# All gathered expert rows of the first tile and of the samples are traced ahead of the gates

## The chip, the core and the metric
The kernel runs on one core of one Trainium2 chip. The metric is device time of one execution in microseconds (us), of which the span, from the first to the last instruction in the trace, is nearly all. VectorE (DVE in the rows), ScalarE (ACT), TensorE (PE), GpSimd (POOL) and the sync engine (SP) each work through their own instructions in a fixed order and wait on semaphores for each other and for DMAs.

## What is computed
One layer of a decoder trunk, for a prompt of 512 tokens (four tiles of 128) and for 32 sample tokens: a projection, two groups of mixing heads, an output projection, and then an expert layer that gives every token 128 of 16384 experts. This last part is where the change lies:

```
def block(hb):
    q = (hb @ w_query).reshape(PEER_BLOCK, PEER_HEADS, 2, D_HALF)
    s = einsum('thcd,cnd->thcn', q, sub_keys)
    s1, i1 = top_k(s[:, :, 0], 16);  s2, i2 = top_k(s[:, :, 1], 16)
    ...                                   # the 16 best sums of s1 and s2: idx (128 per token), gate
    pre = einsum('td,tkd->tk', hb, eu[idx])
    act = gelu(pre) * gate
    return einsum('tk,tkd->td', act, ev[idx])
```

`eu` and `ev` have 16384 rows of 1024 floats each. A final norm gives `y_prompt` and `y_sample`.

## The kernel before
The four prompt tiles are numbered 0 to 3. Tiles 0 and 3 and the 32 samples compute the expert layer **by gathered rows**; tiles 1 and 2 compute it densely, against all 16384 experts.

Gathered rows (`experts`, called by `tile_experts` for a tile and `sample_experts` for the samples): for each k, GpSimd issues an indirect DMA that brings 128 rows of 1024 floats (one expert row to each partition, 512 KB) into one of six `gat` buffers, and VectorE uses it. A row of `eu` is multiplied with the token's vector and summed up (a **dot**: in the trace CUSTOM_DVE_ANT_0, and a short read of the sum into `pre`). After all dots ScalarE computes Gelu over `pre`, and then a row of `ev` is scaled by `act` and added to a running sum `x` (an **add**: SCALAR_TENSOR_TENSOR x<-gat,act,x). A tile has 128 dots and 128 adds. The samples are laid out as 4 groups of 32 tokens on the 128 partitions, so they have 32 dots and 32 adds, and at the end four additions of 32x1024, a norm and an output DMA. In the code `experts` is a generator: each `yield` is one row, and the list `side` holds the generators that are still to run. `beside(n)` adds n to what is due and takes that many steps of `side`.

Dense tiles (1 and 2): first **the gates**. `gates` is called once for each of the two tiles. For 16 groups of 8 tokens VectorE writes one-hot tables `uH` and `uL`, ScalarE scales columns of them into `vH` (line 1441), TensorE multiplies them (line 1444) into a 128x128 matrix of gates for each token, and ScalarE copies that out (lines 1533 and 1543 to 1545). Beside the gates runs `late()`, one step at a time: the output projection and the queries of tile 3 (TensorE, lines 1574 and 1596). Then **the blocks**: 128 of them, each with 128 experts. Each block takes 8 transposes of the `eu` block, 24 matmuls with the tokens, Gelu, the product with the gates, and 24 matmuls with the `ev` block into `acc`; VectorE makes the low halves `uL` and `aL` and the gate products, ScalarE the high halves, GpSimd the low half `vL` (line 1498). Beside the first blocks runs `late_heads()`: the top-16 searches for tile 3, on VectorE. When half of its heads are done it appends tile 3's gathered rows to `side`.

Ahead of the gates the samples' own expert search (`sample_heads`) and the search of tile 2 (`rest(2, dsel[1])`) run on VectorE and GpSimd (top-16 instructions, and products `ce` on GpSimd, line 1053), together with the attention of tile 3 (`attend(3)`).

Where a gathered row is traced is set by three numbers. `AHEAD = 280` steps are traced ahead of the gates: 257 are tile 0 (256 rows and its finish) and 23 belong to the samples. `RATE_G = 0.8` steps are traced after each of the 32 gate groups, 25.6 in all, and what is left goes to the blocks at `RATE_H = 1.6` and `RATE_D = 2.4` a block. The framework's scheduler then fixes the order on every engine; `tc.issue_after(marks[...])` only says that a row may not stand ahead of a given VectorE instruction. VectorE calls go through a recording wrapper, so nearly all of them show its line, 127.

Of the kernel before, what the change touches and what calls it, by code (L numbers as in the profile page):

```python
# [32 lines left out]
LAG = 2  # L33
WST = 3
UV = 5
AHEAD = 280
RATE_G = 0.8
RATE_D = 2.4
RATE_H = 1.6
LATE = 2  # L40
# [69 lines left out]
def bc(ap, shape):  # L110
    return ap.to_broadcast(shape)
# [3 lines left out]
def hymba_step(ctx, tc, x_prompt, x_sample, cache_k, cache_v, state_wkv, state_shift, meta, norm1_g, w_in, mu, w0,  # L115
# [4 lines left out]
    marks = []  # L120
# [124 lines left out]
    side, due = [], [0.0]  # L245

    def beside(n):

        due[0] += n
        while side and due[0] >= 1.0:  # L250
            due[0] -= 1.0
            if next(side[0], None) is None:
                side.pop(0)
        due[0] = min(due[0], 1.0)
# [949 lines left out]
    with ExitStack() as px:  # L1204
# [43 lines left out]
        def put(src, dst):  # L1248

            A.copy(dst[0], src)  # L1250
            V.tensor_tensor(dst[1], src, dst[0].bitcast(F32), OP.subtract)
# [171 lines left out]
    def gates(its, sel, ps, put):  # L1423


        i1T, i2T, gaT = sel
        its, iot = its
        ib = dt_("aH", 2, [128, 2, 128], BF16)
        for c, x in enumerate((i1T, i2T)):
            A.copy(ib[:, c], x)  # L1430
        for n, t8 in enumerate(range(0, 128, 8)):
            ob = dt_("uL", 2, [128, 128, GA], BF16)
            o0, o1 = dt_("uH", 2, [128, 8, 128]), dt_("vH", 2, [128, 8, 128])
            V.tensor_tensor(o0.rearrange("p t j -> p j t"), its, bc(ib[:, 0, t8:t8 + 8].unsqueeze(1), [128, 128, 8]), OP.is_equal)
            V.tensor_tensor(ob, its[:, :, 0:GA], bc(ib[:, 1, t8:t8 + GA].unsqueeze(1), [128, 128, GA]), OP.is_equal)
            for q0 in (0, 4):
                p = ps()
                for q in range(q0, q0 + 4):
                    t = slice(t8 + q, t8 + q + 1)
                    if q < GA:  # L1440
                        A.mul(o1[:, q, :], ob[:, :, q], gaT[:, t])
                    else:
                        V.tensor_scalar(o1[:, q, :], iot, i2T[:, t], gaT[:, t], OP.is_equal, OP.mult)
                    T.matmul(p[:, 128 * (q - q0):128 * (q - q0) + 128], o0[:, q, :], o1[:, q, :], start=True, stop=True)  # L1444
                put(t8 + q0, p)
            if n % LATE:
                next(more, None)
            with tc.issue_after(marks[-1]):
                beside(RATE_G)


    ND = 256
# [3 lines left out]
    def dt_(tag, bufs, shape, dt=F32):  # L1456
        return _t(dn, tag, bufs, shape, dt)
# [158 lines left out]
            yield True  # L1616
        coming[0] = False

    for n in range(AHEAD):
        with tc.issue_after(marks[gather_mark[0]]):  # L1620
            beside(1)
    more = late()
    its = one_hot_table()
    sels = [sel_transposed(0, dps, dt_("selT", 1, [128, 3, 128])), sel_transposed(1, dps, dt_("lsc", 1, [128, 3, 128]))]
    gates(its, sels[0], dps, stage)
    gates(its, sels[1], dps, keep)
    for _ in more:
        pass
# [71 lines left out]
```

## Time and profile before

| what | value |
|---|---|
| median of 3 runs | 2180.15 us (2161.02 to 2190.67) |
| the profiled execution, its own time | 2171.7 us |
| its span | 2169.9 us |
| TensorE busy | 1816.4 us (84%) |
| VectorE busy | 1639.2 us (76%) |
| GpSimd busy | 1271.9 us (59%) |
| ScalarE busy | 862.6 us (40%) |
[...]

All positions are microseconds from the start of the span. The stretches that matter here: the search of tile 2 and the attention of tile 3 up to about 1115, the gates from 1115 to 1248, the blocks from 1248 to about 2129, and the last adds of tile 3 up to the end.

### The profile page before, as it was taken

What the parts mean: (1) busy time and instruction counts of PE and PEld (TensorE: products, weight loads), DVE (VectorE), ACT (ScalarE), POOL (GpSimd) and SP (SyncE); (2) the same over time, 40 slices, a digit from 0 to 9 for tenths busy, and PEclk for the clock granted to TensorE, in tenths of its full rate; (3) what the DMA queues carried; (4) which work ended last, traced back from release to release, by engine and by line L of the source; (5) the groups of instructions that cost most, each with busy time, mean ns of one, the idle gap of its engine ahead of it and who ended that gap; (6) DMA issues with size and microseconds to landing.
All of it is one profiled execution on the core that took longest, in us unless ns stands there. A gap on an engine that the chain in (4) does not pass through costs nothing.

```text
span 2169.9 us, 37101 instructions
## 1 busy us (share of the span) xinstructions
PE 1816.4 (84%) x13915; PEld 1693.1 (78%) x13915; DVE 1639.2 (76%) x3285; ACT 862.6 (40%) x1975; POOL 1271.9 (59%) x951
## 2 busy tenths in 40 slices
PE   5999984585685868898567998999999999999992
PEld 5888973373574757798457988899999999999992
DVE  5643426679878988678989999867676767899988
ACT  6553421221132322433258943444444444444442
POOL 0110103678777677533824365768776777888885
PEclk9999986555675768799769999999999999999996
DMA  7532373487779789966859985789999998999987
GB/s 222 164 107 81 106 199 108 156 304 237 262 247 308 242 282 323 299 222 206 271 182 330 341 287 191 287 297 392 336 336 336 330 338 330 326 322 328 328 312 261
DMA packets 311306, 571.60 MB, mean 263 GB/s; under 512 B 32916, under 2 KB 194694, under 8 KB 310983
## 3 DMA queue, kind: packets, MB, share of 16 engines
q0 software_dynamic: 84048, 305.70, 39.6%
q1 hardware_dynamic: 227078, 263.53, 37.5%
q8 instruction: 110, 1.80, 0.3%
q14 instruction: 70, 0.57, 0.1%
HBM read 544.12 MB, written 25.65 MB: 263 GB/s over the span
## 4 chain that ended last, share of the span: by engine, by line
PE 56%; DVE 17%; issue 9%; DMA 8%; POOL 7%; ACT 3%; SPq 0%; POOLq 0%; DVEq 0%; ACTq 0%
PE acc L1523 5%; PE acc L1524 5%; PE acc L1522 5%; PE w L1508 5%; PE w L1505 5%; PE w L1506 5%; PE w L1491 4%; POOL gat L1075 4%; PE pD L220 3%; DVE x L127 3%; PE pD L966 2%; DVE gat L127 2%; DMA wst<-in_w_query_dram 2%; PE ps L220 2%; PE w L1444 2%
## 5 line engine op out<-in xcount | busy, mean ns | idle before, releaser
L127 DVE SCALAR_TENSOR_TENSOR x<-gat,act,x 128x1024 f32<-128x1024 f32 x287 | 440.5, 1535 | 12.5 <-DMA gat<-in_expert_v_dram,ei 9.4
L1075 POOL DMA_INDIRECT gat<-in_expert_u_dram,ei x256 | 337.0, 1316 | 132.2 <-DVE pre L127 45.8
L1075 POOL DMA_INDIRECT gat<-in_expert_v_dram,ei x256 | 317.7, 1241 | 122.6 <-issue 35.4
L1498 POOL TENSOR_TENSOR vL<-uv,vH 128x1024 fp32r<-128x1024 f32 x128 | 335.2, 2619 | 84.0 <-ACT vH L1497 82.7
L1522 PE MATMUL acc<-aH,vH 128*128 128x256 f32 x1024 | 292.2, 294 | 6.2 <-ACT aH L1514 6.2
L1523 PE MATMUL acc<-aL,vH 128*128 128x256 f32 x1024 | 289.5, 285 | 7.0 <-DVE aL L127 6.8
L1524 PE MATMUL acc<-aH,vL 128*128 128x256 f32 x1024 | 288.6, 284 | 0.0
L1505 PE MATMUL w<-dhH,uH 128*128 128x256 f32 x1024 | 251.6, 283 | 2.7 <-DVE uL L127 1.5
L1506 PE MATMUL w<-dhL,uH 128*128 128x256 f32 x1024 | 251.3, 283 | 0.0
L127 DVE CUSTOM_DVE_ANT_0 gat<-gat,h 128x1024 f32<-128x1024 f32 x160 | 202.7, 1279 | 44.7 <-DMA gat<-in_expert_u_dram,ei 41.7
L1523 PEld LDWEIGHTS acc<-aL,vH 128*128 128x128 f32 x1024 | 197.2, 193 | 8.9 <-DVE aL L127 8.8
L1505 PEld LDWEIGHTS w<-dhH,uH 128*128 128x128 f32 x1024 | 196.7, 192 | 3.1 <-DVE uL L127 1.7
L1522 PEld LDWEIGHTS acc<-aH,vH 128*128 128x128 f32 x1024 | 192.7, 192 | 7.1 <-ACT aH L1514 7.1
L1524 PEld LDWEIGHTS acc<-aH,vL 128*128 128x128 f32 x1024 | 197.1, 192 | 0.0
L1506 PEld LDWEIGHTS w<-dhL,uH 128*128 128x128 f32 x1024 | 196.7, 192 | 0.0
L1497 ACT CAST vH<-uv 128x1024 fp32r<-128x1024 f32 x128 | 134.9, 1054 | 148.9 <-issue 111.3
L127 DVE TENSOR_TENSOR uL<-w,uH 128x512 fp32r<-128x512 f32 x256 | 166.7, 682 | 10.1 <-ACT uH L1493 10.1
L127 DVE TENSOR_TENSOR w<-w,gl 128x128 f32<-128x128 f32 x128 | 50.3, 393 | 148.6 <-ACT w L1509 148.6
L127 DVE CUSTOM_DVE_ANT_0 gat<-gat,lx 128x1024 f32<-128x1024 f32 x128 | 158.1, 1268 | 0.0
L1508 PE MATMUL w<-dhH,uL 128*128 128x256 f32 x1024 | 148.1, 286 | 4.7 <-DVE uL L127 4.3
L1493 ACT CAST uH<-w 128x512 fp32r<-128x512 f32 x256 | 138.0, 593 | 8.0
L1508 PEld LDWEIGHTS w<-dhH,uL 128*128 128x128 f32 x1024 | 133.0, 192 | 7.6 <-DVE uL L127 6.9
(568 smaller groups left out, 4046.5 us busy)
## 6 DMA issues: line engine op xcount, KB each, us to landing
uv<-in_expert_u_dram SPq DMA_DIRECT2D x128, 512.0 KB, 4.5
uv<-in_expert_v_dram SPq DMA_DIRECT2D x128, 512.0 KB, 6.0
wst<-in_w_query_dram SPq DMA_DIRECT2D x48, 512.0 KB, 6.6
wst<-in_w_out_dram SPq DMA_DIRECT2D x24, 512.0 KB
wst<-in_w_in_dram SPq DMA_DIRECT2D x20, 512.0 KB, 4.4
h2T<-in_w_in_dram SPq DMA_DIRECT2D x20, 512.0 KB, 4.2
gscr<-uv SPq DMA_DIRECT2D x10, 1024.0 KB, 5.9
uv<-in_w_query_dram SPq DMA_DIRECT2D x8, 1024.0 KB, 12.2
```

The lines of the kernel that those rows point to most:

```text
L127: r = getattr(nc.vector, name)(*args, **kw)
L220: T.matmul(p[:, 0:n], w[:, k, :], x, start=(k == 0 and x is H and w is wH), stop=(k == 7 and w is wL))
L1075: G.indirect_dma_start(out=r, out_offset=None, in_=w[0], in_offset=bass.IndirectOffsetOnAxis(ap=ei[:, k:k + 1], axis=0))
L1493: A.copy(uH[:, ks, :], p)
L1497: A.copy(vH, vn)
L1498: G.tensor_tensor(vL, vn, vH.bitcast(F32), OP.subtract)
L1505: T.matmul(pre, uH[:, k, :], hH[:, k, :], start=(k == 0), stop=False)
L1506: T.matmul(pre, uH[:, k, :], hL[:, k, :], start=False, stop=False)
L1508: T.matmul(pre, uL[:, k, :], hH[:, k, :], start=False, stop=(k == 7))
L1522: T.matmul(o, vH[:, ds_], aH, start=(j == 0 and d % 2 == 0), stop=False, skip_group_check=True)
L1523: T.matmul(o, vH[:, ds_], aL, start=False, stop=False, skip_group_check=True)
L1524: T.matmul(o, vL[:, ds_], aH, start=False, stop=(j == 127), skip_group_check=True)
```

## The change
The constant `AHEAD` becomes "until nothing is left": all 257 steps of tile 0 and all 65 of the samples are traced before the first gate. After the gate groups no row is traced any more. The blocks' rates stay; since `side` is empty when they begin, they trace no row until `late_heads` appends tile 3.

```diff
-AHEAD = 280
-RATE_G = 0.8
 RATE_D = 2.4
 RATE_H = 1.6
...
             if n % LATE:
                 next(more, None)
-            with tc.issue_after(marks[-1]):
-                beside(RATE_G)
...
-    for n in range(AHEAD):
+    while side:
         with tc.issue_after(marks[gather_mark[0]]):
             beside(1)
     more = late()
```

Lines move up by two, and by four further down (a VectorE row shows L125 where it showed L127). On VectorE the two programs have the same order up to the 1326th row, which the trace has at about 1064 us. On TensorE the order is the same up to the blocks.

**First place, VectorE ahead of the gates.** Before, in the search of tile 2 (`sco`, `vals`, `cand` are its tiles) and the softmax of tile 3 (`sD`), no gathered row stands:

```order
L127 MATCH_REPLACE sco_1436_6944<-vals_7008,sco_1436_6944 128x128 x4
L127 TENSOR_TENSOR sD_7799<-sD_7799,sD_7804 128x4
L127 MATCH_REPLACE sco_1456_7044<-vals_7105,sco_1456_7044 128x128 x4
L127 MAX vals_7008<-sco_1436_6944 128x8 x4
L127 RECIPROCAL sD_7808<-sD_7799 128x4
L127 MAX vals_7105<-sco_1456_7044 128x8 x4
L127 MAX_INDEX idxu_7005<-vals_7008,sco_1436_6944 128x8 x4
```

Now a dot of the samples (the two ISA rows are the dot and the reading of its sum) stands between each two of these on VectorE:

```order
L125 MATCH_REPLACE sco_1436_6944<-vals_7008,sco_1436_6944 128x128 x4
L125 ISA gat_8780,pre_8703<-gat_8780,h_1918_8698 128x1024
L125 ISA pre_8703 128x1
L125 MATCH_REPLACE sco_1456_7044<-vals_7105,sco_1456_7044 128x128 x4
L125 ISA gat_8783,pre_8703<-gat_8783,h_1918_8698 128x1024
L125 ISA pre_8703 128x1
L125 TENSOR_TENSOR sD_7804<-sD_7797,snk 128x4
L125 ISA gat_8786,pre_8703<-gat_8786,h_1918_8698 128x1024
L125 ISA pre_8703 128x1
L125 MAX vals_7008<-sco_1436_6944 128x8 x4
```

Eleven dots, the product of `act`, the first scaling and 20 adds have moved into this stretch, all ahead of the first gate instruction.

**Second place, VectorE at the first gates.** Before, the last search rows (`ce`, `dsel`) are followed by the low halves of tiles 1 and 2 (`dhL`) and then by the one-hot tables:

```order
L127 TENSOR_TENSOR ce_7171<-iota_87,hl_7152 128x512
L127 TENSOR_REDUCE dsel_17_112<-ce_7171 128x32
L127 TENSOR_TENSOR dhL<-w_7873,dhH 128x4x128
L127 TENSOR_TENSOR dhL<-w_7880,dhH 128x4x128
L127 TENSOR_TENSOR dhL<-w_7889,dhH 128x4x128
L127 TENSOR_TENSOR dhL<-w_7896,dhH 128x4x128
L127 TENSOR_SCALAR vH_8792<-aL_8771,selT_8775 128x128 x2
L127 TENSOR_TENSOR uH_8791<-vL_8773,aH_8787 128x128x8
```

Now, on VectorE at the same place, adds of the samples stand between them, and some are left behind the first gate instruction:

```order
L125 TENSOR_TENSOR dhL<-w_7873,dhH 128x4x128
L125 SCALAR_TENSOR_TENSOR x_1953_8803<-gat_8859,act_8800,x_1953_8803 128x1024
L125 TENSOR_TENSOR dhL<-w_7880,dhH 128x4x128
L125 SCALAR_TENSOR_TENSOR x_1953_8803<-gat_8862,act_8800,x_1953_8803 128x1024
L125 TENSOR_TENSOR dhL<-w_7889,dhH 128x4x128
L125 TENSOR_TENSOR dhL<-w_7896,dhH 128x4x128
L125 TENSOR_SCALAR vH_8950<-aL_8929,selT_8933 128x128
L125 SCALAR_TENSOR_TENSOR x_1953_8803<-gat_8865,act_8800,x_1953_8803 128x1024
L125 TENSOR_SCALAR vH_8950<-aL_8929,selT_8933 128x128
L125 TENSOR_TENSOR uH_8949<-vL_8931,aH_8945 128x128x8
```

Eleven adds, the samples' four closing additions and their norm still stand among the groups of the first dense tile; where before 11 dots, the first scaling and 13 adds stood among both tiles' groups, none stands now among those of the second tile.

**Third place, VectorE in the first blocks.** Before, adds of the samples stand between the low halves and gate products of the blocks:

```order
L127 TENSOR_TENSOR uL_10185<-w_10186,uH_10184 128x512
L127 TENSOR_TENSOR uL_10185<-w_10193,uH_10184 128x512
L127 SCALAR_TENSOR_TENSOR x_2051_9243<-gat_10004,act_9240,x_2051_9243 128x1024
L127 TENSOR_TENSOR aL_10178<-w_10149,aH_10177 128x256
L127 SCALAR_TENSOR_TENSOR x_2051_9243<-gat_10066,act_9240,x_2051_9243 128x1024
L127 TENSOR_TENSOR w_10250<-w_10250,gl_10115 128x128
L127 TENSOR_TENSOR w_10250<-w_10250,gA_7907 128x128
```

Now VectorE has there only the blocks' own rows and the search of tile 3 (`lvals`, `lsc`, `lidx`):

```order
L125 TENSOR_TENSOR w_10228<-w_10228,gl_10194 128x128
L125 TENSOR_TENSOR w_10228<-w_10228,gA_7907 128x128
L125 TENSOR_TENSOR uL_10264<-w_10265,uH_10263 128x512
L125 TENSOR_TENSOR uL_10264<-w_10272,uH_10263 128x512
L125 TENSOR_TENSOR aL_10257<-w_10228,aH_10256 128x256
L125 MAX lvals_10666<-lsc_10664 128x8 x4
L125 MAX_INDEX lidx_10309<-lvals_10666,lsc_10664 128x8 x4
```

Eighteen adds and the samples' finish have left the blocks. GpSimd's and SP's queues move with them: the 64 gathers of the samples now all stand ahead of the first `vL` on GpSimd, and the output DMA of the samples stands on SP between the sixth and the seventh write of gates to `gscr`, where it stood among the blocks' loads. From about the 17th block on the rows of tile 3 stand at the same blocks as before.

## Rows read from the trace of the kernel before

**Rows 1.** Span and mean granted TensorE clock of the core.

```profile
core 0: 2169.9 us, clock 0.866
```

**Rows 2.** Busy time by stretch: PE, PEld, DVE, ACT, POOL, then PEclk, DMA share, GB/s.

```profile
670.00:960.00 290.00, 239.61 (x1433) 202.37 (x1433) 239.80 (x383) 91.37 (x229) 186.53 (x166) 0.74 0.86 284
...
1064.20:1115.10 50.90, 24.64 (x126) 19.87 (x124) 44.58 (x155) 12.23 (x32) 25.85 (x26) 0.60 0.62 193
...
1112.00:1180.00 68.00, 49.27 (x317) 45.37 (x318) 61.36 (x97) 56.75 (x141) 22.11 (x12) 0.86 0.83 277
1180.00:1248.00 68.00, 67.46 (x571) 65.02 (x570) 62.65 (x80) 64.46 (x231) 26.70 (x14) 1.00 0.95 327
1248.00:1400.00 152.00, 134.77 (x1065) 129.85 (x1064) 144.96 (x369) 64.93 (x123) 95.92 (x76) 0.97 0.71 249
1400.00:2100.00 700.00, 699.56 (x5904) 698.46 (x5903) 542.80 (x868) 295.35 (x530) 543.46 (x324) 1.00 0.91 333
```

**Rows 3.** What VectorE waited for from 1018 to 1112: us, times, longest.

```profile
DVE dsel L127 <- POOL ce L1053: 5.6, 4, 1.7
DVE gat L127 <- DMA gat<-in_expert_u_dram,eis: 2.7, 2, 2.2
```

**Rows 4.** Adds of tile 0, 670 to 960: busy us, mean ns, idle before.

```profile
L127 DVE SCALAR_TENSOR_TENSOR x<-gat,act,x 128x1024 f32<-128x1024 f32 x127 | 170.5, 1342 | 8.3 <-DMA gat<-in_expert_v_dram,ei 7.4
```

**Rows 5.** Dots of the samples from 1018 to 1112, grouped as above.

```profile
L127 DVE CUSTOM_DVE_ANT_0 gat<-gat,h 128x1024 f32<-128x1024 f32 x21 | 31.7, 1515 | 2.7 <-DMA gat<-in_expert_u_dram,eis 2.7
...
L127 DVE DVE_READ_ACCUMULATOR2_ANT pre<- 128x1 f32 x21 | 1.6, 78 | 0.0
```

**Rows 6.** Rows of the samples among the gates, 1112 to 1248.

```profile
L127 DVE SCALAR_TENSOR_TENSOR x<-gat,act,x 128x1024 f32<-128x1024 f32 x13 | 16.7, 1281 | 0.0
L127 DVE CUSTOM_DVE_ANT_0 gat<-gat,h 128x1024 f32<-128x1024 f32 x11 | 13.3, 1214 | 0.0
...
L127 DVE TENSOR_SCALAR x<-gat,act 128x1024 f32<-128x1024 f32 x1 | 0.7, 749 | 0.0
```

**Rows 7.** Rows of the samples among the blocks, 1248 to 1400.

```profile
L127 DVE SCALAR_TENSOR_TENSOR x<-gat,act,x 128x1024 f32<-128x1024 f32 x18 | 35.3, 1964 | 0.0
...
L127 DVE TENSOR_TENSOR h<-h,gat 32x1024 f32<-32x1024 f32 x3 | 4.8, 1584 | 0.4 <-DMA gat<-x 0.4
...
L127 DVE SCALAR_TENSOR_TENSOR gat<-h,sF,gat 32x1024 f32<-32x1024 f32 x1 | 1.3, 1262 | 0.0
```

**Rows 8.** GpSimd's low halves from 1248 to 1400.

```profile
L1498 POOL TENSOR_TENSOR vL<-uv,vH 128x1024 fp32r<-128x1024 f32 x19 | 46.8, 2464 | 18.2 <-ACT vH L1497 18.1
```

**Rows 9.** Gathers of the samples, 1018 to 1115: ns min/median/max, first and last start.

```profile
L1075 POOL DMA_INDIRECT gat<-in_expert_u_dram,eis x27: 934/981/2004, 1021.2 to 1087.1; - x27
...
DMA to landing us min/median/max: 4.3/5.6/9.5
```

**Rows 10.** What VectorE waited for from 1112 to 1180.

```profile
DVE uL L127 <- ACT vH L1441: 2.9, 2, 1.6
DVE act L127 <- ACT act L1089: 2.2, 1, 2.2
```

**Rows 11.** The chain that ended last, later gates: start us, us, what.

```profile
1207.80 1.79 PE w L1444 x16
1209.59 1.56 PE w L1596 x14
...
1211.37 2.15 PE w L1596 x18
```

**Rows 12.** Matmuls with the low half, 8 a block, 1264 to 1399.4.

```profile
L1508 PE MATMUL w<-dhH,uL x138: 274/283/388, 1264.6 to 1399.4; 128*128 128x256 f32 x138
```

**Rows 13.** The chain that ended last, two blocks behind 1399.

```profile
1399.44 0.96 PE w L1508 x8
...
1406.06 0.96 PE w L1508 x8
```

**Rows 14.** DMA issues of the page: count, KB each, us to landing.

```profile
uv<-in_w_query_dram SPq DMA_DIRECT2D x8, 1024.0 KB, 12.2
```

## The prediction
> **What bounds the kernel now.** I read the busy times by stretch first and asked of each stretch which engine is full. Between 1064 and 1115, the search of tile 2 ahead of the gates, VectorE is busy for 44.58 of 50.9 us and TensorE for half of it [rows 2]: VectorE sets the pace, and its few waits are for GpSimd's products and for gathered data, 5.6 and 2.7 us in the 94 us from 1018 [rows 3]. The first half of the gates (1112 to 1180) is mixed: VectorE 61.36, ScalarE 56.75, TensorE 49.27 of 68 us. The second half (1180 to 1248) is full on TensorE, 67.46 of 68 us at the whole granted clock, 1.00 [rows 2]; there the chain that ended last runs from matmul to matmul, gates (line 1444) and late queries (line 1596) by turns [rows 11]. In the first blocks (1248 to 1400) VectorE is full again, 144.96 of 152 us, and from 1400 to 2100 TensorE is, 699.56 of 700 us, with VectorE at 78% [rows 2]. So a gathered row costs time ahead of the gates, in the gates' first half at most partly, in their second half nothing, and in the first blocks time again.
>
> How much the first blocks lose can be counted. Two full blocks are 6.62 us apart [rows 13]. From 1264.6 to 1399.4 there are 138 of the matmuls that come eight to a block, 17 block distances and the start of one more [rows 12]. At full pace they would take 17 x 6.62 = 112.5 us; they took 134.8. **22.3 us** is what the blocks can give back at most.
>
> **The change part by part.** Up to the 1326th VectorE instruction nothing moves, so the first 1064 us stay.
>
> *Ahead of the gates.* Eleven dots come in at 1.515 + 0.078 us [rows 5], 17.5 us; the first scaling at 0.75 us [rows 6]; 20 adds, taken at the 1.342 us that tile 0's adds had beside similar work [rows 4], 26.8 us; the small product of `act`, some 0.2. Together 45.3 us on the engine that sets the pace here, where before the gathers of these rows waited. What can cover them is the 6.3 us that VectorE idles in this stretch [rows 2]: the adds now stand between a product and its sum, where the wait for GpSimd is. If all of it is filled, the stretch grows by 39 us; if VectorE is kept as busy as now (87.6%), by 45.3/0.876 = 52 us; if only as busy as from 670 to 960, where adds stood beside other work (239.8 of 290 us, 82.7%), the 89.9 us of both take 108.7, 58 us more. I take 93%, because the rows fill waits but bring waits for their data: 89.9/0.93 = 96.7, **+46 us**. Data should nearly keep up. 27 gathers were issued here before, the first at 1021 and each landing some 5.6 us later [rows 9]; some 31 more of 0.52 MB make 16 MB, and the stretch moved 193 GB/s at a DMA share of 0.62 [rows 2]. At 284 GB/s, as from 670 to 960, 10 + 16 MB take 92 us, just the stretch's new length. GpSimd's in-order queue must pass the gathers before the products `ce` behind them, and each gather waits until one of six buffers is free.
>
> *The gates.* Eleven dots (11 x 1.29 = 14.2 us), the scaling (0.75) and 13 adds (16.7) leave [rows 6]. Eleven adds (14.1), four additions and the norm's last product (4 x 1.5 + 1.3 = 7.3, at their prices in the blocks [rows 7]) come into the first half. In the first half that is +7 us of VectorE work, less the 2.2 us in which VectorE waited for the samples' Gelu and the 2.9 us for ScalarE's columns [rows 10], which other rows then fill. The second half loses adds on an engine that was not the bound. I take **0**, with +6 if the first half waits for VectorE alone, and -11 if it falls to ScalarE's 56.75 us. On SP the samples' output DMA waits for the end of that norm, and behind it wait a load of query weights and two writes of gates. The load takes 12.2 us [rows 14]; the scheduler has it beside the norm of tile 3, whose matmuls need the weights later, so it is at nothing here, 5 us if the norm comes late.
>
> *The blocks.* Eighteen adds leave at 1.964 us, 35.3 us, and the finish with 4.8 + 1.2 + 1.3 us [rows 7]: VectorE falls from 145 to 102 us over about 20 blocks, which need 132 us of TensorE. On average that is the 78% at which TensorE ran full later. It isn't spread evenly: tile 3's search remains, and it stands in the first 17 blocks. So not all of 22.3 us comes back; I take **-17 us**, between -10 and -22.
>
> That an add costs 1.96 us in the blocks and 1.28 us in the gates [rows 6, 7] goes with GpSimd's `vL`, 19 instructions of 2.46 us in the blocks [rows 8] and none in the gates. [...]
>
> From the blocks' 20th on and in the tail, tile 3's rows stand at the same blocks, so nothing changes.
>
> **Sum:** +46 + 0 - 17 = **+29 us**. The profiled execution took 2171.7 us, 1.8 us more than its span [rows 1], and 8 us less than the median of the three runs, 2180.15. The mean of the four is 2176; on that I get **2205 us**, 1.3% more. I take 2% (43 us) as what a measurement of this kernel can tell from no change, so the forecast is "within 2%, on the slow side".
>
> **The rivals.** (1) *GpSimd's queue throttles the stretch ahead of the gates.* The search of tile 2 goes from VectorE to GpSimd and back for each `ce`, and gathers that wait for a buffer now stand in front of these products; VectorE's next row waits for the product, the buffer for VectorE. If VectorE's busy share falls to 80%, the stretch takes 112 us, +61; with -17 in the blocks that is +44, and from there on the kernel is slower by over 2%: 2220 us, and 2226 at 76%. For it speaks that from 670 to 960 it ran at 82.7% with mostly adds; against it, that dots were as dense from 1018 on and VectorE waited only 2.7 us for their data [rows 3].
>
> (2) *The rows go into gaps and both later stages give back all.* The stretch grows by 39, the gates fall to ScalarE's time (-11), the blocks give 22: +6 us, 2182 us. For it speaks that the gates' first half has three engines below 91%. To be faster than before it needs 6 us more, for instance adds at 1.28 us in place of 1.342 and dots at 1.29 in place of 1.59, as in the gates, which are 4.5 us: it ends at about no change, and a gain of 2% is out of reach, since 39 us stand against 33.
>
> (3) *The change hardly does what it says*, because the scheduler puts the rows where VectorE is free anyway. In part that is so, 11 adds still stand among the gates. But 31 rows and the scaling have moved ahead, so this alone gives no zero.
>
> **How the numbers follow.** The forecast, between +15 and +43 us, has 0.60; rival 1 has 0.18; rival 2, from +15 down to somewhat below zero, 0.20; 0.02 is left for a gain of over 2% by something that I don't see. Faster by over 2%: 0.02; within 2%: 0.80; slower: 0.18. The low bound of the sum is 39 - 11 - 22 = +6, the high one 58 + 6 + 5 - 10 = +59; with the runs' own scatter (2161 to 2191) beside it, leaving out a tenth at each end, the range is 2174 to 2232 us.
>
> **What would show it.** Right: the gates (from about 1115 before) beginning some 46 us later, VectorE over 90% busy ahead of it; the gates as long as before; 6.62 us a block nearly from the second block on, with adds of the samples nowhere among them; the same 770 us from the 20th block to the end. Wrong: a gate stage shorter by over 10 us; a stretch ahead of the gates in which VectorE waits for gathers or `ce` by tens of microseconds; blocks that lose 20 us even without the adds, because tile 3's search is what held them.

## The result, and the profile after

The changed kernel took 2200.85 us (median of 4 runs, 2195.3 to 2207.6) against 2177.06 us of the kernel before on the same chip (4 runs, 2161.02 to 2190.67). The ratio is 1.0148, with a 95% interval of 1.0113 to 1.0183: slower, by less than the 2% that was set as "no change". The profiled execution took 2202.21 us with a span of 2200.4 us, 30.5 us more than the span of before [rows 1].

To see where the 30.5 us are, both traces are cut at the same instructions: the VectorE row at which the two orders begin to differ (a sum `sD<-ax`), the first gate column `vH<-aL` on VectorE, the product that ends tile 3's norm (`lx<-lx,sE,uv`, between the gates' two halves), the last gate matmul, and the first and the last block matmul with the low half. Lengths in us:

| stretch | before | after | difference | predicted |
|---|---|---|---|---|
| up to `sD<-ax` | 1083.5 | 1082.5 | -1.0 | 0 |
| ahead of the gates | 31.6 | 67.6 | +36.0 | +46 |
| gates, first half | 55.7 | 65.6 | +9.9 | 0 for both halves |
| gates, second half | 76.1 | 76.6 | +0.5 | |
| last gate to first block | 6.9 | 10.0 | +3.1 | (not named) |
| blocks | 864.0 | 845.1 | -18.9 | -17 |
| tail | 52.1 | 53.0 | +0.9 | 0 |
| sum | 2169.9 | 2200.4 | +30.5 | +29 |

The windows of the changed kernel over these stretches (without the first) show what filled them; the columns are those of [rows 2].

```profile
1082.50:1150.10 67.60, 15.55 (x62) 12.06 (x62) 64.28 (x167) 13.70 (x31) 57.37 (x49) 0.50 0.93 329
1150.10:1215.70 65.60, 43.95 (x256) 40.47 (x256) 60.53 (x82) 48.16 (x125) 12.70 (x11) 0.79 0.81 246
1215.70:1292.30 76.60, 74.75 (x615) 72.49 (x616) 51.75 (x72) 68.38 (x239) 0.00 (x0) 0.96 0.66 215
1302.30:1448.00 145.70, 143.28 (x1197) 142.26 (x1197) 107.58 (x327) 65.48 (x117) 81.12 (x62) 1.00 0.63 225
1448.00:2147.40 699.40, 698.90 (x5895) 697.59 (x5894) 547.04 (x863) 293.38 (x526) 543.68 (x325) 1.00 0.91 331
```

Ahead of the gates VectorE is busy 64.28 of 67.6 us, 95%, where the kernel before had 26.23 of 31.6 us, in the first of these rows; the other two are the halves of its gates:

```profile
1083.50:1115.10 31.60, 15.82 (x62) 11.92 (x62) 26.23 (x123) 9.11 (x24) 10.88 (x16) 0.50 0.67 211
1115.10:1170.80 55.70, 39.61 (x256) 36.51 (x256) 52.69 (x84) 47.67 (x122) 20.19 (x10) 0.90 0.79 261
1170.80:1246.90 76.10, 74.22 (x615) 71.95 (x616) 68.49 (x89) 69.70 (x241) 28.61 (x17) 0.97 0.96 331
```

So VectorE took 38.1 us more and idled 2.1 us less, which is the +36.0. But DMA at 0.93 and GpSimd at 57.4 us are nearly full too, so the window alone doesn't tell which of them set the length. The groups of that stretch, and what VectorE waited for in it:

```profile
L125 DVE SCALAR_TENSOR_TENSOR x<-gat,act,x 128x1024 f32<-128x1024 f32 x20 | 27.1, 1357 | 1.0 <-DMA gat<-in_expert_v_dram,eis 0.9
L125 DVE CUSTOM_DVE_ANT_0 gat<-gat,h 128x1024 f32<-128x1024 f32 x12 | 14.5, 1214 | 0.0
...
DVE dsel L125 <- POOL ce L1051: 2.3, 2, 1.2
DVE x L125 <- DMA gat<-in_expert_v_dram,eis: 0.9, 2, 0.6
```

The wait for `ce` products, 5.6 us in the 94 us from 1018 on before [rows 3], didn't grow: it is 3.3 us from 1018 to 1150.1. In the gates' first half the chain that ended last runs through VectorE, then ScalarE, and ends with tile 3's norm:

```profile
1174.53 1.94 DVE uH L125
...
1181.62 1.12 DVE h L125
...
1188.60 1.14 DVE h L125
...
1201.93 1.28 ACT L196
...
1208.20 2.15 ACT vH L1439 x6
...
1215.68 1.28 DVE lx L125
```

`h` are two of the four additions that close the samples; they stand inside the chain, ahead of `lx`. The L196 row is a table load on ScalarE in front of the square roots of both norms, the samples' and tile 3's; the kernel before has one of the same 1.28 us there for tile 3's norm alone. In the window from 1150.10 no engine is quite full: VectorE 92%, TensorE 67% at a granted clock of 0.79.

In the blocks TensorE is full almost from the first one on. The low-half matmuls, eight a block:

```profile
L1504 PE MATMUL w<-dhH,uL x176: 278/283/415, 1302.3 to 1442.7; 128*128 128x256 f32 x176
```

These are 22 whole blocks: 21 distances and the eight matmuls of the last, about 0.9 us, in 140.4 us, which makes (140.4 - 0.9)/21 = 6.64 us a block. Before, 134.8 us for 17 distances were 7.93 us each [rows 12]; the full pace is 6.62 us [rows 13].

### The profile page after: what moved, and what is told of

Its sections match the earlier page's. It is cut to its first block, busy times and chain, and to the rows that moved or that the text cites. A ratio compares the mean times of both kernels' runs of the same rounds, so it can differ in the third digit from the quotient of the medians.

```text
span 2200.4 us, 37107 instructions
## 1 busy us (share of the span) xinstructions
PE 1815.7 (83%) x13915; PEld 1697.0 (77%) x13915; DVE 1626.7 (74%) x3285; ACT 863.8 (39%) x1976; POOL 1249.8 (57%) x951
## 4 chain that ended last, share of the span: by engine, by line
PE 55%; DVE 16%; issue 10%; POOL 8%; DMA 7%; ACT 4%; SPq 0%; POOLq 0%; DVEq 0%; ACTq 0%
POOL gat L1073 5%; PE w L1504 5%; PE w L1501 5%; PE w L1502 5%; PE acc L1520 5%; PE acc L1518 5%; PE acc L1519 5%; PE w L1487 4%; DVE x L125 3%; PE pD L218 3%; DMA wst<-in_w_query_dram 3%; PE pD L964 2%; DVE gat L125 2%; PE ps L218 2%; PE w L1442 2%
## 5 line engine op out<-in xcount | busy, mean ns | idle before, releaser
L125 DVE SCALAR_TENSOR_TENSOR x<-gat,act,x 128x1024 f32<-128x1024 f32 x287 | 429.4, 1496 | 14.5 <-DMA gat<-in_expert_v_dram,ei 9.3
L1073 POOL DMA_INDIRECT gat<-in_expert_u_dram,ei x256 | 329.4, 1287 | 138.0 <-issue 45.1
L125 DVE CUSTOM_DVE_ANT_0 gat<-gat,h 128x1024 f32<-128x1024 f32 x160 | 201.1, 1270 | 39.1 <-DMA gat<-in_expert_u_dram,ei 33.4
L125 DVE TENSOR_TENSOR w<-w,gl 128x128 f32<-128x128 f32 x128 | 50.4, 394 | 171.0 <-ACT w L1505 170.1
L125 DVE TENSOR_TENSOR uL<-w,uH 128x512 fp32r<-128x512 f32 x256 | 166.9, 684 | 4.4 <-ACT uH L1489 3.9
L125 DVE CUSTOM_DVE_ANT_0 gat<-gat,lx 128x1024 f32<-128x1024 f32 x128 | 154.5, 1241 | 0.0
```

Of the source, the lines that this page charges most:

```text
L125: r = getattr(nc.vector, name)(*args, **kw)
L1073: G.indirect_dma_start(out=r, out_offset=None, in_=w[0], in_offset=bass.IndirectOffsetOnAxis(ap=ei[:, k:k + 1], axis=0))
```

## The experiments

The kernel before was timed beside each of them on the same chip and took 2165 to 2168 us there; where an expectation speaks of 2177 us, the ratio counts. The place where the orders begin to differ stood between 1067 and 1099 us in these traces, so traced executions differ by up to 32 us, 16 either way of the 1083 of the kernel before, for reasons that lie ahead of the change; traces are compared by the lengths of their stretches, kernels by their ratios.

**The samples' closing moved out of the gates** (e1):

```diff
-    while side:
+    for n in range(321):
```

> The changed kernel, but the last step of the samples (their last two adds, the four additions, the norm, the output) is traced beside the blocks and not ahead of the gates. The changed kernel took 2201 us; its gates were 13.5 us longer than before, and VectorE had the samples' closing norm (at 1214.5) right in front of the norm of tile 3 (1215.7), with TensorE half idle from 1200 to 1220. Theory A, the samples' closing stands in VectorE's and ScalarE's queues ahead of tile 3's sums and norm, and late() waits for those: the gates shorten by 9 to 13 us, the blocks take the closing for 0 to 5 us, 2188 to 2197 us. Rival B, the hole is tile 3's own norm with its table loads, which the gates must wait for whatever stands beside it: the gates stay as long and the blocks get the closing, 2200 to 2206 us.

Ratio 1.0116 (1.0075 to 1.0157), 2191.14 us. The first half:

```profile
1143.30:1203.90 60.60, 41.69 (x256) 38.26 (x256) 52.61 (x74) 46.37 (x117) 10.05 (x6) 0.84 0.78 243
```

5.0 us shorter than the 65.6, and the blocks 2.1 us longer (847.2). The two intervals overlap, so by times alone this is not settled; by the stretches it lies between A's 9 and B's 0. TensorE's hole at the norm is still there (it waits 7.5 us for `lx`; 8.5 in the changed kernel and 7.4 already before), so that hole isn't the closing's doing, and A's reading of it falls.

**Only half of the change: all the rest beside the gates** (e2), **beside the blocks** (e3), **beside the gates' second half** (e6). In each the loop ahead of the gates is the old one, and one line differs:

```diff
-    while side:
+    for n in range(280):
...
 # e2, in gates():
+            with tc.issue_after(marks[-1]):
+                beside(1.33)
 # e3: nothing
 # e6, in gates():
+                beside(0 if put is stage else 2.63)
```

> 280 steps ahead of the gates as in the kernel before, and all 42 others beside the gates (1.33 a group instead of 0.8), so none is left for the blocks: the half of the change that frees the blocks, without the half that loads the stretch ahead of the gates. Kernel before: 2177 us. Theory A, a row costs its 1.2 to 1.3 us wherever VectorE is the full engine, and nothing only while TensorE leaves it room (75.0 - 67.3 = 7.7 us in the gates' second half): first half 8 rows more, +10; second half 8 rows and the closing (7.3 us) more, 17.5 us against 7.7, +10; blocks -19; 2178 us (2170 to 2186). Rival C, the second half is bound by TensorE and swallows them: +10 - 19, 2168 us.

> 280 steps ahead of the gates as in the kernel before, none beside the gates, the other 42 steps beside the first blocks. Kernel before: 2177 us. Theory A, the blocks lost time to the samples' rows on VectorE (the change gave back 18.9 us for 18 adds and the closing, 1.0 us for each row and less than its 1.96 us of VectorE time): 24 rows more in the blocks cost +25 to +35, the gates' first half gives back up to 9; 2193 to 2203 us, about as slow as the changed kernel. Rival D, it is tile 3's search that holds the first blocks and the rows fit beside it: +5 - 9, 2170 to 2175 us.

> 280 steps ahead of the gates as in the kernel before, none beside the gates' first half, the other 42 (2.63 a group) beside the second half. Kernel before: 2177 us. Theory A, VectorE has 7.7 us of room in the second half: first half -9, second half 29 rows and the closing more, 44 us against 7.7, +37, blocks -19; 2186 us (2178 to 2192). Rival C, the second half is TensorE's and rows beside it cost nothing, as the prediction took it: -9 - 19, 2149 us, which would be faster than both kernels by over 1%.

e2: ratio 1.0027 (1.0006 to 1.0049). e3: 1.0221 (1.0177 to 1.0266), the slowest of all. e6: 1.0009 (0.9983 to 1.0034). All three have the 31.6 or 31.7 us ahead of the gates that the kernel before has, so the +36.0 us belong to the rows traced there and to nothing else. The halves of the gates, first e3's two, then the second one of e2 and of e6:

```profile
1113.70:1166.20 52.50, 38.63 (x256) 35.96 (x256) 42.30 (x65) 47.41 (x122) 0.00 (x0) 0.89 0.66 197
1166.20:1243.30 77.10, 75.22 (x615) 72.95 (x616) 51.77 (x71) 68.35 (x239) 0.00 (x0) 0.95 0.66 216
```

```profile
1170.50:1260.80 90.30, 78.12 (x616) 76.31 (x617) 87.14 (x103) 71.36 (x244) 44.95 (x27) 0.90 0.95 341
```

```profile
1183.00:1269.00 86.00, 77.45 (x616) 75.32 (x617) 78.40 (x107) 72.88 (x246) 41.51 (x24) 0.92 0.92 322
```

The second half took 77.1 us with no row (e3), 76.1 with 13 adds and a dot (before), 86.0 with 12 adds and 11 dots (e6), 90.3 with 30 adds (e2). It is TensorE's for the first 13 adds. By 30 it is nearly VectorE's, as A had it: in e8 below, with the same rows, VectorE is busy for 87.21 of 87.7 us and waits for no gathered row.

```profile
1179.90:1267.60 87.70, 78.17 (x616) 76.28 (x617) 87.21 (x103) 71.28 (x244) 46.69 (x27) 0.91 0.98 351
```

The 2.6 us that e2 has on top go with query weights that come late: TensorE waits 4.7 us for them in e2 and 1.9 us in e8. The intervals of e2 and of e6 lie above C's 0.996 and 0.987; C falls. e2's first half is 60.8 us, 5.1 more than before for the same instructions and one dot. e6 came out at the low end of A's range, since only 12 of its adds stand there: the order has 19 and the closing among the first blocks, though they were traced beside the gates.

e3 is slower than A said (1.022 where 2193 to 2203 us is 1.007 to 1.012), and its reason is another one; D falls too. The blocks did not grow: 862.0 us from the first to the last low-half matmul, with 42 rows of the samples ahead of tile 3's, against 864.0. The tail did:

```profile
2115.20:2210.90 95.70, 9.76 (x66) 8.98 (x65) 81.05 (x70) 12.08 (x31) 64.12 (x54) 0.57 0.85 313
```

```profile
L125 DVE SCALAR_TENSOR_TENSOR x<-gat,act,x 128x1024 f32<-128x1024 f32 x56 | 74.7, 1334 | 7.4 <-DMA gat<-in_expert_v_dram,ei 6.1
```

56 adds of tile 3 stand behind the last block, 26 before and after the change (35.2 us). `side` is worked off in order, so tile 3's rows wait for the samples': the first dot of tile 3 comes 218.5 us after the first block, 121.1 us before.

**The price of a row ahead of the gates: its VectorE time, or its data?** e4 cuts the adds of the samples to an eighth of the columns; e5 leaves out three of four of the gathers for them; e10 does both. All three leave part of the samples' sum out, so they stand for time alone.

```diff
 # e4, in add():
+            elif fresh:
+                V.scalar_tensor_tensor(acc[:, 0:128], v[:, 0:128], act[:, k:k + 1], acc[:, 0:128], OP.mult, OP.add)
 # e5, in rows():
+                if not (fresh and w is ev and k % 4):
-                r = gat()
+                    r = gat()
```

> The changed kernel with the samples' adds cut to the first 128 of 1024 columns (the rest of the samples' expert sum is left out); all gathers are made in full. In the changed kernel the stretch from the row that both orders share to the first gate is 67.6 us, with 64.3 us of VectorE, 20 of these adds at 1.357 us, and a DMA share of 0.93; the gates' first half has 11 more. Theory A, VectorE's time is the price: the stretch loses some 20 us, the gates' first half some 10; the ratio to the kernel before falls from 1.015 to 0.998 to 1.003. Rival E, the data set the pace (0.93 of 67.6 us, so at most 5 us to gain in the stretch, 5 in the half): 1.009 to 1.012.

> The changed kernel with every fourth gather of the samples' 32 adds only: four adds use one gathered row buffer, so 24 gathers of 0.5 MB are left out (and the sum is made of fewer rows); VectorE's work is unchanged. Theory A, VectorE's time is the price: the stretch ahead of the gates stays within 3 us of 67.6, the ratio to the kernel before is 1.012 to 1.016. Rival E, the data set the pace: with half of the stretch's bytes gone it shrinks by 10 us or more, 1.005 to 1.010.

> The changed kernel with both cuts at once: the samples' adds over 128 of 1024 columns, and every fourth of their gathers only (their expert sum is left incomplete). Each cut alone moved the stretch ahead of the gates little: 67.6 us in the changed kernel, 63.0 us with short adds (VectorE busy 47.0 and waiting 15.3 us for gathered rows), 65.1 us with few gathers (VectorE busy 64.9). Theory H, VectorE's work and the arrival of the gathered rows each need nearly the whole stretch, so only both cuts free it: 48 to 53 us, the gates' first half 54 to 58 instead of 65.6, a ratio to the kernel before of 1.000 to 1.005. Rival I, something that neither cut touches holds it too (the search of tile 2 going from VectorE to GpSimd and back): 60 us or more, 1.006 to 1.009.

Ratios: e4 1.0086 (1.006 to 1.0111), e5 1.0105 (1.0057 to 1.0154), e10 1.0038 (1.0009 to 1.0067). The stretch ahead of the gates and the first half, for e4, e5 and e10:

```profile
1084.70:1147.70 63.00, 15.29 (x62) 12.11 (x62) 47.03 (x168) 12.80 (x29) 49.76 (x50) 0.50 0.92 335
1147.70:1207.50 59.80, 41.10 (x256) 38.74 (x256) 50.19 (x81) 48.68 (x129) 6.59 (x10) 0.84 0.90 285
```

```profile
1067.30:1132.40 65.10, 15.55 (x62) 12.06 (x62) 64.92 (x167) 13.60 (x31) 36.58 (x30) 0.50 0.64 214
1132.40:1191.10 58.70, 39.34 (x256) 36.50 (x256) 58.49 (x80) 47.89 (x120) 2.65 (x5) 0.88 0.68 202
```

```profile
1072.00:1125.80 53.80, 15.30 (x62) 12.11 (x62) 52.59 (x180) 12.13 (x27) 33.87 (x34) 0.53 0.83 267
1125.80:1181.30 55.50, 40.52 (x256) 36.81 (x256) 46.42 (x70) 49.30 (x130) 0.54 (x1) 0.90 0.66 202
```

With short adds VectorE has 17.3 us less to do, and the stretch shrinks by 4.6: in place of the work stands a wait for the gathered rows.

```profile
DVE x L125 <- DMA gat<-in_expert_v_dram,eis: 15.3, 15, 2.0
```

With few gathers the DMA share falls from 0.93 to 0.64 and the stretch shrinks by 2.5 us, VectorE busy for 64.92 of 65.1. With both it shrinks by 13.8 us, although all 31 adds and one of the closing additions now fit into it (20 and none in the changed kernel). So theory A and rival E were both half right, E on the stretch of e4 (at most 5 us to gain) and A on that of e5 (within 3 us): VectorE's work and the rows' arrival each need about the whole stretch. I, with 60 us or more, falls. H has the half and the ratio right, and the stretch is 0.8 us above its 48 to 53, with more work in it than H reckoned with. The first half of the gates shrinks as well, from 65.6 to 59.8, 58.7, and 55.5 with both, but not in the same way: there each cut alone gives back more than half of what both do.

**Two steps of tile 3's search a block**, in the changed kernel (e7), with a later start (e14), and with the rest of the samples beside the gates (e8, e13, e15):

```diff
         mid = nxt
-        next(more, None)
+        for _ in range(2):            # e14: 2 if j else 0
+            next(more, None)
 # e8:  280 steps ahead, beside(1.33) in gates()
 # e13: 280 steps ahead, beside(0.8 if put is stage else 1.83)
 # e15: 280 steps ahead, beside(0.8 if put is stage else 1.2)
```

> The changed kernel with two steps of tile 3's search a block instead of one. In the changed kernel VectorE is busy for 104 of the first 139 us of the blocks, and yet the tail is as long as before (53.0 and 52.1 us, 26 adds of tile 3 behind the last block in both). Theory F, the freed VectorE time earns more only if tile 3's rows begin sooner: its first dot comes 103 us after the first block, and its 128 dots take 413 us, 3.2 us each; if the search ends some 8 blocks sooner, the rows begin some 50 us sooner and some 16 adds of 1.35 us leave the tail, -20 us, a ratio of 1.003 to 1.008. Rival G, search and rows are held by GpSimd's products or by the gathers and not by where their steps are traced: ratio 1.012 to 1.017 as for the changed kernel.

> The changed kernel with two steps of tile 3's search a block, the first of them behind the second block and not the first. Without samples' rows VectorE takes the search's first row at the end of the gates and waits there for its scores from memory (4.9 us in the changed kernel, from 1291.7 on), with the first blocks' low halves behind it: 10 us lie between the last gate and the first block's last product, 5 to 7 us where rows of the samples stood in between. Theory M, the in-order wait is the whole of that difference: 5 to 6 us, a ratio 0.002 below the 1.006 of the kernel without this edit. Rival N, the blocks wait for their transposes and high halves anyway: 10 us, 1.005 to 1.008.

> The kernel that had 280 steps ahead of the gates and the other 42 beside the gates (ratio 1.003 to the kernel before), with two steps of tile 3's search a block. Theory F: its blocks hold hardly any row of the samples, so the search has room as in the changed kernel, and the same 20 us come back: a ratio of 0.992 to 0.996, faster than both kernels. Rival G: 1.000 to 1.005.

> 280 steps ahead of the gates; 0.8 a group beside the gates' first half as in the kernel before, 1.83 beside the second half, so none of the samples is left for the blocks; two steps of tile 3's search a block. Against the kernel with 1.33 in both halves and the same search (0.997): in that one the first half took 60.9 us where the kernel before has 55.7 with nearly the same instructions on VectorE, at a DMA share of 0.82 against 0.79. Theory J, the gathers come too densely for the loads of the output weights: the first half gets back its 5 us, the second stays near 88 to 90 us; a ratio of 0.993 to 0.997, faster than both kernels. Rival K, the denser gathers only move into the second half, which grows by the same 5 us: 0.996 to 1.000.

> As the kernel with 0.8 and 1.83 a group and the dense search, but 1.2 beside the gates' second half, so some 10 rows of the samples and their closing are left for the first blocks. The second half has room for some 18 rows beside TensorE (76 to 77 us with 0 and with 13 rows, 87.7 and 90.3 us with 30). Theory A: the second half takes 77 to 81 us, 8 to 10 us less, and the blocks take 10 rows more at 1.0 us: the same total, a ratio of 0.993 to 0.997. Rival L, the rows in the blocks push tile 3's rows back and come out in the tail at 1.35 us and more, as 24 rows did (tail 95.7 us): 0.998 to 1.004.

e7: ratio 1.0062 (1.0037 to 1.0087), in F's range. The first dot of tile 3 comes 59.4 us after the first block (103.3 in the changed kernel), nine adds stand behind the last block, and the tail takes 30.9 us in place of 53.0; the blocks take 852.1, 7.0 us more.

```profile
L125 DVE CUSTOM_DVE_ANT_0 gat<-gat,lx x128: 1206/1217/4064, 1357.0 to 1768.5; 128x1024 f32<-128x1024 f32 x128
...
L125 DVE SCALAR_TENSOR_TENSOR x<-gat,act,x 128x1024 f32<-128x1024 f32 x9 | 14.3, 1586 | 0.1
```

e14 did not do what it was made for: the order still has the search's first row ahead of the first block's low halves, and the wait there is as before. The stretch from the last gate to the first block is 9.9 us, as in e7, so M and N stay open. Its ratio is 1.0034 (1.0001 to 1.0067).

```profile
DVE lvals L125 <- DMA lsc<-lscr: 4.9, 1, 4.9
```

e8: 0.9972 (0.9941 to 1.0002), which is 0.55% below e2 (F), but above F's range and not told apart from the kernel before; its tail is 31.0 us and its blocks 865.8, so 12.9 of the 21 us went back into the blocks. e13: 0.9986 (0.9958 to 1.0014), K's range. The first half has its 55.7 us again, as J said, and the second takes 82.5; but nine adds of the samples were pushed behind the last gate, and the blocks take 876.6 us. Why they take 10.8 us more than those of e15, which has eleven adds there, isn't shown. e15: **0.9928 (0.9902 to 0.9955), 2155.68 us, faster than both kernels,** than the kernel before by 0.7%, which is less than 2% and yet clear of the interval. Its halves:

```profile
1113.00:1168.60 55.60, 39.94 (x256) 36.37 (x256) 52.56 (x84) 47.34 (x122) 19.36 (x10) 0.87 0.79 260
1168.60:1250.40 81.80, 74.57 (x615) 72.48 (x616) 75.51 (x96) 70.87 (x243) 41.30 (x21) 0.96 0.95 335
```

20 adds and a dot in the second half cost 5.7 us over before, the blocks 1.8 us (865.8), and the tail gives back 15.3 (36.8 us, 15 adds behind the last block): L, rows of the samples coming out in the tail, falls for this search. The gain over the kernel before is thus in the tail, where the denser search gave 22.1 us back in e7 and 21.1 in e8 against e2; that most of it is the search's is argued from these and not shown, since that search in the kernel before, with nothing else changed, wasn't tried.

## Why the prediction held, point by point

The direction and the two large terms, ahead of the gates and in the blocks, were right. That the sum came so close (+29 against +30.5 us) is luck, by errors that cancel: ahead of the gates 10 us too much, at the gates and their end 13.5 us too little.

**The place.** The prediction, and the section on the change, have the point from which the orders differ at about 1064 us. The last row that both share starts at 1083.5 us. What the rows moved into is a stretch of 31.6 us with 5.4 us of VectorE idle time, not one of 50.9 with 6.3.

**Ahead of the gates: +36.0, not +46.** The step that failed is the size of the added work: 45.3 us were taken, VectorE's busy time grew by 38.1. A dot took 1.214 us and not 1.515; eleven dots make 3.3 us of the difference. The adds were sized right, 1.357 against 1.342 us. The other 4 us are in the main that the traced durations of VectorE's rows overlap at their ends (by 6.1 us in all in this stretch before, by 9.7 after), which the prediction added up in full: in the chain of waits, a dot counts 1.13 us. The busy share was to be 93% and is 95%. That data would "nearly keep up" is what e4, e5 and e10 showed, and more exactly than it was meant: at 67.6 us the rows' arrival was itself within 5 us of being the bound. The adds did not come out at the 1.96 us that they have in the blocks, where `vL` stands beside them [rows 7, 8]: 19 of the 20 took 1.25 to 1.29 us and one, with a `ce` product beside it, 2.91. Five such products stood in the stretch; of the four that start within an add, three took 1.55 to 1.62 us and the one in the long add 1.28, where the five of the same stretch before took 1.26 to 1.27.

**The gates: +10.4, not 0.** The second half was as predicted, +0.5 us: these rows beside a full TensorE were free, and taking them away gives nothing back. The other runs bound the statement: 13 adds and a dot are free, 20 adds and a dot cost 5.7 us (e15), 12 adds and 11 dots 9.9 (e6), 30 adds 11.6 and 14.2 (e8, e2). The cost begins before VectorE fills the half: in e15 it is busy for 75.51 of 81.8 us and TensorE for 74.57, with the DMA share at 0.95, and which of their waits makes the 5.7 us isn't shown. The first half is the step that failed. It was to lie between ScalarE's time (-11) and VectorE's (+6). Without any row it takes 52.5 us (e3), so -3.2 was its real floor: 10 dots had cost only 3.2 us there in the kernel before. Above it, the changed kernel's rows cost 13.1 us. Short adds give back 5.8 of these, few gathers 6.9, and both together, with which all adds go ahead of the gates, 10.1; 3.0 us are left, with most of the closing. VectorE's added work was sized about right (+7 forecast, 7.8 measured). What the prediction had left out is that the gathers themselves cost time there: it weighed the adds in the gates by VectorE time alone, which gave at most +6. It isn't the double bound of the stretch ahead, where each cut alone gave little; what the gathers delay in this half isn't shown.

**SP and the end of the samples' norm** were taken at nothing, 5 us if late. Moving the closing away gained 5.0 us in the half (e1), with two of the adds in it; whether SP's wait had a part in that was not separated.

**The start of the blocks, +3.1 us**, has no step in the prediction. With no row of the samples in between, VectorE's order has the search of tile 3 first, which waits 4.9 us for its scores, and the first block's low halves stand behind it. The traces divide by this order: 9.8 to 10.0 us with the search first (the changed kernel, e1, e3, e4, e5, e7, e10, e14), 5.2 to 6.9 with an add of the samples there and the low halves next (before, e2, e6, e8, e13, e15). That the wait makes the 3.1 us is likely by this and not shown by a change of it alone, since e14 failed to move it.

**The blocks: -18.9, predicted -17.** The 22.3 us that the count of distances gave as the most were nearly all given back, 6.64 us a block from the first one on, although tile 3's search stayed where it was. The prediction's reason, VectorE overloaded over the first 20 blocks, is only part of it: e3 put 24 more rows there, the blocks didn't grow (862.0 us against 864.0), and the bill came in the tail (95.7 us against 52.1). So a row in the blocks cost block time or delayed tile 3's rows.

**The tail: 0, measured +0.9**, 26 adds in both. It stayed because tile 3's rows begin at the same block; e7 shows that the freed VectorE time was worth another 15 us to whoever began them sooner.

**The rivals.** Rival 1 would have had VectorE's share fall to 80% behind GpSimd's queue. It was 95%, and the wait for `ce` 2.3 us. Rival 2 needed both later stages to give back all; the blocks nearly did, the gates took. Rival 3: the rows did move.

## What to carry to other kernels

Price a moved row by the stage that it enters and the stage that it leaves, and count there both what computes it and what brings it: where the two need the same time, removing either alone may show next to nothing, and only removing both shows the price (here 4.6 and 2.5 us for either, 13.8 for both). Time freed on an engine in one stage is worth something only if the next thing in line may start sooner; look for what is traced at a fixed place behind it (here a search, one step a block: at two steps the tail fell from 53.0 to 30.9 us in e7). Here rows beside a full TensorE were free only up to a point, and the busy share of their own engine would have put that point too far: 13 adds cost nothing, while 20 cost 5.7 us with VectorE at 92% (e15).

## What the runs showed of the hardware

A gather's issue on GpSimd took longer beside full adds on VectorE, in a way that neither busy column shows: 1.265 us in the mean beside these (27 of them ahead of the gates in the changed kernel), 1.019 us beside adds of an eighth the width (28 in e4):

```profile
L1073 POOL DMA_INDIRECT gat<-in_expert_v_dram,eis x27 | 34.1, 1265 | 8.1 <-issue 4.3 <-DMA gat<-in_expert_v_dram,eis 1.2 <-DVE idxu L125 0.3
```

```profile
L1073 POOL DMA_INDIRECT gat<-in_expert_v_dram,eis x28 | 28.5, 1019 | 11.1 <-DVE x L125 6.4 <-DVE sel L125 0.9 <-DVE hl L125 0.8
```

27 times the difference is 6.6 us of GpSimd's time in this stretch. The single rows show how it comes about:

```profile
1133.34 1.27 DVE L125 SCALAR_TENSOR_TENSOR x<-gat,act,x 128x1024 f32<-128x1024 f32 x1
1133.98 1.44 POOL L1073 DMA_INDIRECT gat<-in_expert_v_dram,eis  x1 [0.30 <-issue]
```

The add ends at 1134.61, the issue 0.81 us behind it. In the whole trace of the changed kernel 156 gathers start while an add of any tile runs, and 150 of them end 0.75 to 0.90 us after that add's end; they start at any point of it and take 0.94 to 2.02 us, while the 26 beside which VectorE does nothing take 0.93 to 0.98 us. In these 150 rows the issue was done only after the add had ended; of the other six, three were done 0.32 to 0.34 us ahead of the add's end and three 0.95 to 1.42 us behind it. Beside another instruction of VectorE it looks alike: in the kernel before, the 13 gathers that start beside a one-hot table (TENSOR_TENSOR uH<-vL,aH, 128x1024) took 2.26 to 2.35 us and ended 0.68 to 0.75 us after it.

TensorE's granted clock fell three times within the gates of the changed kernel: for 6.8 us from 1170.5, for 6.8 us from 1201.2 and for 10.2 us from 1211.4. The kernel before has one fall, of 6.8 us from 1168.9, and e5 one. The first of the three stands where VectorE, full, holds TensorE up:

```profile
1160.10:1165.10 5.00, 5.00 (x32) 4.62 (x31) 5.00 (x7) 5.00 (x14) 3.15 (x3) 0.99 0.76 209
1165.10:1170.10 5.00, 3.30 (x26) 2.91 (x24) 5.00 (x7) 4.70 (x13) 2.76 (x1) 1.00 1.01 303
1170.10:1175.10 5.00, 2.86 (x11) 2.71 (x12) 4.93 (x6) 1.19 (x3) 0.00 (x0) 0.54 0.95 292
1175.10:1180.10 5.00, 5.00 (x24) 4.32 (x23) 5.00 (x8) 1.97 (x6) 0.00 (x0) 0.78 0.88 244
...
PE w L1442 <- DVE lx L125: 3.8, 1, 3.8
```

The clock is 0.99 and 1.00 up to 1170.1, with TensorE busy for 3.30 us of the last 5, and 0.54 in the 5 us behind; over the 6.8 us from 1170.5 alone it is 0.50. From 1175.1 on TensorE is busy for all of 5 us, and the clock of these is 0.78. The wait is for the first of tile 3's four sums, which VectorE reaches behind three adds of the samples; the kernel before and e5 have no such wait.

The 256 matmuls of the first half took 43.95 us of TensorE time at a granted clock of 0.79, in place of the 38.63 of e3, whose clock was 0.89 there. How much of that lengthened the half isn't separated.
